# pb rows 2 to 7 as seven block products for eight, in a fp32 gated decoder step on one core

## The chip, the cores and the metric

One NeuronCore of a Trainium2 chip runs the kernel; the seven other cores are idle. The metric is device time in microseconds, from one launch. Engines are named TensorE (PE, its weight loads PEld), VectorE (DVE), ScalarE (ACT), GpSimd (POOL) and SyncE (SP, which only issues DMAs).

## The reference, cut to what matters

One layer of a hybrid decoder on 1024 prompt tokens and 8 sample tokens (T = 1032 columns), model width 1024, all in fp32:

```
z = h @ w_in;  u, v, g_a, x_b, g_b, z_a, z_b = split(z)
y_a = chunk_spatial_gate(u, rmsnorm(v)) * silu(g_a)
y_b = rg_lru(conv(x_b)) * silu(g_b)
merged = sigmoid(z_a) * (y_a @ w_pa) + sigmoid(z_b) * (y_b @ w_pb)
out = x + gate * (merged @ w_out);  y = rmsnorm(out)
```

`pb` is the product y_b @ w_pb, `pa` is y_a @ w_pa. Each is 1024 x 1024 by 1024 x 1032.

## The kernel before

Everything is held transposed: 128 channels on the partitions, 1032 tokens along the row. A fp32 operand is split in two fp32r parts, hi (a copy by ScalarE) and lo (the difference, by VectorE), and a product is three matmuls: hi·hi, hi·lo, lo·hi. Tokens lie in two halves of HT = 516 columns, each in two quarters of QW = 258.

The stages in order: the v columns of w_in; then 24 **units** (R for x_b and g_b, Z for z_a and z_b, G for u and g_a; eight of each); then pb row by row, then pa with the products of the gate between its first rows, then w_out.

A unit computes two rows of 128 output channels by a scheme with seven block products for eight: two row blocks, two halves of the contraction, two halves of the tokens. The right-hand operands of the seven products p1 to p7 are the blocks A11, A12, A22 of h and four sums S1 to S4, held in `HF`. The left-hand ones are raw weight blocks or sums of them, made by GpSimd in `sums` four stages ahead and split in `prep` two stages ahead. One product is a **stage**: `seven`, 24 matmuls of 258 columns. Results are put together by `evac` one stage later (`later`). The first unit, R0, runs its stages in another order (`FIRST`) with a fourth pair of PSUM banks.

All engines run in program order through the units (`in_order`, class `InOrder`). Side work is hung on stage numbers with `at(stage, f, ...)`: the recurrent chain (`recurrent`), the spatial gate (`spatial`), the silu's, and the spills. y_rnn(i) makes y_b's channel block i in the tile `scan_out[i, "g"]` (`gr`). For i < NSPLIT = 4 it is split at once, by y_hi in `scan_out[i]` and by y_lo in `gr` itself, and both halves are stored in DRAM as `ybs`; blocks 4 to 6 are stored whole as `ybd`; block 7 stays. Late in G7 GpSimd's queue loads the ybs tiles back, SyncE's the ybd tiles.

After the units the PSUM pool of bank pairs is closed (`new_phase`) and one of eight single banks is opened. `do_pb(m)` takes row m of pb: `product` runs three column chunks of CH = 344 with 24 matmuls each, VectorE multiplies each by sigmoid(z_b) in `sb`, and the row is stored as `mbd`. `do_pa(m)` does the same with `ya` and adds mbd's row. These rows are ordered by the list `ops`, and the weights of an op are loaded one op and split one op ahead (`fetch_load`, `fetch_split`).

SBUF tiles of one row (1032 fp32) come from one ring of NSLOT = 36 `slots`; half rows from five buffers of `half_tile`; weight blocks from `wst` (4 raw, 3 split).

Of the kernel before, what the change touches and what calls it, by code (L numbers as in the profile page):

```python
# [8 lines left out]
F32 = mybir.dt.float32  # L9
# [44 lines left out]
def tile_hybrid_step(  # L54
# [734 lines left out]
    def spill(tag):  # L789
# [21 lines left out]
    units.append(("G", KT - 1))  # L811
    pos = {u: 7 * n for n, u in enumerate(units)}
    pairs = {"R": (O_XB, O_GB), "Z": (O_ZA, O_ZB), "G": (O_U, O_GA)}
    wr, wfs = {}, {}

    def load_unit(u):
        kind, m = u
        out = []
        for j, off in enumerate(pairs[kind]):
            raw = wst[0].tile([P, 2, HD], F32, tag="raw", name=f"raw_{kind}{m}_{j}", bufs=4)  # L820
            c0 = off + m * P
            last_w[0] = S.dma_start(
                out=raw[:].rearrange("p a (k n) -> p (a k) n", n=P),
                in_=win[:, c0 : c0 + P].rearrange("(k p) n -> p k n", p=P),
            ).ins
            out.append(raw)
        wr[u] = out

    def sums(u, f):
        rx, ry = wr[u][0:2]  # L830
        first = u == units[0]
        if f == ("p4" if first else "p6"):
            t = wst[0].tile([P, 2, HD], F32, tag="wt", name=f"wt_{u[0]}{u[1]}", bufs=1)
            wr[u].append(t)
            G.tensor_tensor(t[:, 0], ry[:, 0], rx[:, 0], ALU.subtract)
            G.tensor_tensor(t[:, 1], ry[:, 1], t[:, 0], ALU.subtract)
            if first:
# [46 lines left out]
    FIRST = ("p1", "p4", "p2", "p6", "p5", "p7", "p3")  # L884
    stages = [(u, f) for u in units for f in (FIRST if u == units[0] else FORMS)]
    later = []
    side = {}

    def ahead(n, step):
        if n < len(stages):  # L890
            step(*stages[n])

    def unit(n0, u, use):
        name = f"{u[0]}{u[1]}"
        first = u == units[0]
        pa_, pb_, pc_ = (pair_bank(f"{n}_{name}") for n in "abc")
# [30 lines left out]
        for j, f in enumerate(FIRST if first else FORMS):  # L927
# [357 lines left out]
    def y_rnn(i):  # L1285
# [83 lines left out]

    def do_pb(m, w):  # L1370
        sb = slot(f"sb{m}")
        with tc.issue_after(last_w[0]):
            nc.sync.dma_start(out=sb, in_=zbd[m])
        for ps, sl in product(f"pb{m}", w, yb):
            V.tensor_tensor(sb[:, sl], ps, sb[:, sl], ALU.mult)
        nc.sync.dma_start(out=mbd[m], in_=sb)

# [18 lines left out]
    wsrc = {"pa": (w_pa[0], 0), "pb": (w_pb[0], 0)}  # L1396
    todo = list(ops)
# [22 lines left out]
    def fetch_split():  # L1420
# [3 lines left out]
        if kind == "gate":  # L1424
            hi, lo = (slot(f"gw{i}_{j}", [P, D], F32R) for j in range(2))
        elif kind == "pb" and i < 2:
            hi, lo = (slot(f"pb{i}_{j}", [P, KT, P], F32R) for j in range(2))
        else:
# [38 lines left out]
    def recurrent(i):  # L1467
# [23 lines left out]
        for t, step in zip(when, steps):  # L1491
            at(n + t, chain, i, step)
        if not last:
            at(n + 23, y_rnn, i)
        if i < NSPLIT:
# [64 lines left out]

    acts = {"pa": do_pa, "pb": do_pb, "gate": do_gate}
    for kind, i in ops:
        fetch_load()
        if (kind, i) != ("pb", 0):
            fetch_split()
        if (kind, i) == ("pb", 1):
            do_states(0, None)
        if kind == "pb" and i > 1:
            for k in {2: (0,), 3: (1,), 4: (2,), 5: (3,), 6: (4, 5), 7: (6, 7)}[i]:
                y_load("ya", yad, ya, k)  # L1570
                y_split("ya", ya, k)
        if (kind, i) == ("pa", KT - 1):
# [119 lines left out]
```

## Time and profile before

| | |
|---|---|
| median of 3 runs | 968.83 us (967.47 to 969.25) |
| the profiled execution, its own time | 965.57 us |
| its span, first to last instruction | 963.9 us |
| mean granted TensorE clock | 0.995 |
| TensorE busy | 940.5 us, 98% |
| VectorE, ScalarE, GpSimd busy | 645.2, 499.7, 228.1 us |
| units | 144.0 to 667.3 us |
| pb | 670.1 to 761.1 us |
| pa and gate products | 761.1 to 859 us |

The times below are microseconds from the start of the span of that one execution. A TensorE that is 98% busy says that nearly all other work is hidden under it; where it does wait, the profile names who released it.

### The profile page before, as it was taken

How to read it: one execution, taken by the hardware profiler on the slowest of the kernel's cores; microseconds unless marked ns; L12 is line 12 of the kernel's file. 1: busy time of each engine (PE TensorE's matmuls, PEld its weight loads, DVE VectorE, ACT ScalarE, POOL GpSimd, SP SyncE). 2: the span in 40 equal slices, each digit the busy share in tenths (PEclk: the TensorE clock that was granted, in tenths of full speed). 3: DMA queues.
4: the chain of work that ended last, by engine and by line, in shares of the span. 5: the costliest groups of instructions: out<-in, count | busy, mean ns of one | idle time of the engine just before them, and what ended most of it. 6: DMA issues, size and time to landing. Idle time of an engine off the chain costs nothing. (4 is left out here: it accounts for less than half of the span.)

```text
span 963.9 us, 16594 instructions
## 1 busy us (share of the span) xinstructions
PE 940.5 (98%) x6575; PEld 878.1 (91%) x6575; DVE 645.2 (67%) x972; ACT 499.7 (52%) x810; POOL 228.1 (24%) x170
## 2 busy tenths in 40 slices
PE   7999999999999999999999999998999999999996
PEld 3778779899999999999999999998999999997785
DVE  3886877869578587696785875969443356555544
ACT  4674446584774865846748558467122233222212
POOL 1142443233242252342422523322000000000001
PEclk9999999999999999999999999999999999999998
DMA  9952103243143163241430622518774465334321
GB/s 288 294 174 65 68 35 110 66 114 120 45 141 116 33 180 88 76 156 47 141 94 23 199 57 67 170 34 301 275 279 168 156 220 202 130 109 154 110 85 49
DMA packets 127942, 126.27 MB, mean 131 GB/s; under 512 B 10502, under 2 KB 105278, under 8 KB 127856
## 3 DMA queue, kind: packets, MB, share of 16 engines
q1 hardware_dynamic: 126648, 120.96, 39.5%
q0 software_dynamic: 1216, 4.24, 1.3%
q8 instruction: 52, 0.85, 0.4%
q14 instruction: 26, 0.21, 0.1%
HBM read 93.92 MB, written 31.33 MB: 130 GB/s over the span
## 5 line engine op out<-in xcount | busy, mean ns | idle before, releaser
L45 PE MATMUL v<-wv,h 128*128 128x512 f32 x384 | 97.1, 401 | 2.8 <-ACT junk L45 2.1
L45 PE MATMUL ps_pb<-ybh,pb 128*128 128x344 f32 x384 | 91.1, 320 | 2.8 <-issue 2.8
L45 PE MATMUL ps_pa<-yah,pa 128*128 128x344 f32 x384 | 91.4, 320 | 0.0
L45 PEld LDWEIGHTS v<-wv,h 128*128 128x128 f32 x384 | 69.6, 188 | 20.8 <-ACT junk L45 2.5
L45 POOL TENSOR_TENSOR rs_o<-ms_o,nhalf 128x1 f32<-128x1 f32 (+1 forms) x9 | 8.0, 894 | 296.3 <-DVE ms_o L45 296.3
L45 PEld LDWEIGHTS ps_pb<-ybh,pb 128*128 128x128 f32 x384 | 66.4, 188 | 3.0 <-issue 3.0
L45 PEld LDWEIGHTS ps_pa<-yah,pa 128*128 128x128 f32 x384 | 66.4, 188 | 0.5
L45 PE MATMUL ps_pb<-ybl,pb 128*128 128x344 f32 x192 | 61.4, 320 | 0.0
L45 PE MATMUL ps_pa<-yal,pa 128*128 128x344 f32 x192 | 61.4, 320 | 0.0
L45 PE MATMUL o<-wol,mgh 128*128 128x512 f32 x128 | 50.5, 395 | 0.2 <-DVE wol L45 0.2
L45 DVE SCALAR_TENSOR_TENSOR xc<-xb,vec,xc 128x512 f32<-128x512 f32 x48 | 50.3, 1049 | 0.6
L45 PE MATMUL o<-woh,mgh 128*128 128x512 f32 x128 | 50.4, 394 | 0.0
L45 PE MATMUL o<-woh,mgl 128*128 128x512 f32 x128 | 50.4, 394 | 0.0
L45 ACT ACTIVATE mgh<-sa 128x344 fp32r<-128x344 f32 x24 | 11.7, 490 | 63.2 <-DVE sa L45 59.5
L45 ACT ACT_TABLE_LOAD x34 | 43.6, 1283 | 1.4 <-PEq L1676 0.8
L45 DVE TENSOR_TENSOR sb<-ps_pb,sb 128x344 f32<-128x344 f32 x24 | 12.4, 516 | 46.3 <-PE ps_pb L45 46.3
L45 ACT ACTIVATE junk<-xr 128x512 bf16<-128x512 f32 (+2 forms) x19 | 11.6, 608 | 56.8 <-DVE xr L45 51.4
L45 POOL TENSOR_TENSOR wt_R<-raw_R,raw_R 128x512 f32<-128x512 f32 x8 | 16.9, 2106 | 97.2 <-DVE wf_Z1p L45 15.1
L45 PEld LDWEIGHTS ps_pa<-yal,pa 128*128 128x128 f32 x192 | 36.1, 188 | 0.2
L45 PEld LDWEIGHTS ps_pb<-ybl,pb 128*128 128x128 f32 x192 | 36.1, 188 | 0.0
L45 POOL TENSOR_TENSOR wt_R<-raw_R,wt_R 128x512 f32<-128x512 f32 x15 | 33.1, 2209 | 8.6 <-DVE wf_R6p L45 1.1
L45 POOL TENSOR_TENSOR wt_Z<-raw_Z,raw_Z 128x512 f32<-128x512 f32 x8 | 10.8, 1351 | 98.9 <-DVE l L45 14.2
(535 smaller groups left out, 2554.0 us busy)
## 6 DMA issues: line engine op xcount, KB each, us to landing
raw_ada<-in_w_ada_dram SPq DMA_DIRECT2D x32, 256.0 KB
raw_R<-in_w_in_dram SPq DMA_DIRECT2D x16, 512.0 KB
raw_Z<-in_w_in_dram SPq DMA_DIRECT2D x16, 512.0 KB
raw_G<-in_w_in_dram SPq DMA_DIRECT2D x16, 512.0 KB
zad<-za SPq DMA_DIRECT2D x16, 258.0 KB
yad<-t SPq DMA_DIRECT2D x8, 516.0 KB
sb<-zbd SPq DMA_DIRECT2D x8, 516.0 KB
yar<-yad SPq DMA_DIRECT2D x8, 516.0 KB
```

Source lines behind the costliest of these rows:

```text
L45: ins = f(*args, **kwargs)
```

## The change

- The eight rows of pb become four pairs. Rows 0 and 1 (unit C0) are computed in full, with 258 columns a matmul, in eight stages of 24 matmuls: four outputs (two rows, two halves) over contraction blocks 0 to 3, then the same four over blocks 4 to 7. Rows 2 to 7 (units B1 to B3) are computed as the units are, by seven products; B1 in the order of `FIRST`.
- Rows 0 and 1 of pa (unit C1) are computed as C0 is, after B3. Rows 2 to 7 of pa and the gate products stay as they are, after the change of PSUM pools, which now follows C1.
- The operands of pb are tiles of one block and one half with hi and lo side by side (`ya_tile`), and are at once A11, A12 and A22 of the seven products. `ybs` is stored in that order. S1 to S4 are new (`y_sums`, `y_form`), from fp32 blocks that are loaded back (`yb_raw`), so that ybd is stored for blocks 0 to 6; `y_lo` writes into `scan_out[i]` where it wrote into `gr`.
- Loads and splits of the operands, ya's too, are hung on stages by hand.

The diff, cut to its core:

```diff
-    ybs = { (i, j): drm.tile([P, T], ...) for i in range(NSPLIT) for j in range(2) }
+    ybs = [
+        drm.tile([P, 2, 2, HT], F32, tag=f"ybs{i}", name=f"ybs{i}") for i in range(NSPLIT)
+    ]
...
+    units += [("C", 0), ("B", 1), ("B", 2), ("B", 3), ("C", 1)]
+    pos = {}
+    for u in units:
+        pos[u] = sum(8 if v[0] == "C" else 7 for v in pos)
+    OPENERS = (units[0], ("B", 1))
...
-                x = HF[XOF[f], kp]
+                x = (YF if u[0] == "B" else HF)[XOF[f], kp]
...
+    def classical(n0, u, w, ys, use):
+        ps = [pair_bank(f"{u[0]}{u[1]}_{q}") for q in range(4)]
+        for j in range(8):
+            q, part = j % 4, j // 4
...
+            hi, lo = w[q // 2]
+            for k in range(4 * part, 4 * part + 4):
+                xh, xl = ys(k, q % 2)
...
+                    for i, (a, b) in enumerate(((hi, xh), (hi, xl), (lo, xh))):
+                        TE.matmul(ps[q][:, c, 0:QW], a[:, k % 2, ks], b[:, sl],
...
+            if part:
+                later.append(lambda q=q: use(q // 2, q % 2, ps[q][:, :, 0:QW]))
...
-        if NSPLIT <= i < KT - 1:
+        if i < KT - 1:
             later.append(lambda: S.dma_start(out=ybd[i], in_=gr))
 
     def y_hi(i):
         A.activation(scan_out[i][:].bitcast(F32R), scan_out[i, "g"], AF.Copy)
-        S.dma_start(out=ybs[i, 0], in_=scan_out[i][:])
+        S.dma_start(out=ybs[i][:, :, 0, :], in_=h2(scan_out[i][:]))
 
     def y_lo(i):
         gr = scan_out[i, "g"]
-        V.tensor_tensor(gr[:].bitcast(F32R), gr, scan_out[i], ALU.subtract)
-        S.dma_start(out=ybs[i, 1], in_=gr)
+        V.tensor_tensor(scan_out[i][:], gr, scan_out[i], ALU.subtract)
+        S.dma_start(out=ybs[i][:, :, 1, :], in_=h2(scan_out[i][:]))
...
+    def yb_parts(k):
+        for half in range(2):
+            G.dma_start(out=ya_tile(k, half), in_=ybs[k][:, half])
+    def yb_raw(k):
+        yraw[k] = slot(f"ybr{k}")
+        S.dma_start(out=yraw[k], in_=ybd[k])
+    def yb_split(k):
+        for half in range(2):
+            t = ya_tile(k, half)
+            split(t[:, 0], t[:, 1], yraw[k][:, half * HT : (half + 1) * HT])
+    def y_sums(kp, eng):
+        x, y = yraw[2 * kp], yraw[2 * kp + 1]
+        x0, x1, y0, y1 = x[:, 0:HT], x[:, HT:T], y[:, 0:HT], y[:, HT:T]
+        eng.tensor_tensor(y1, x1, y1, ALU.add)
+        eng.tensor_tensor(x1, x0, x1, ALU.subtract)
+        eng.tensor_tensor(x0, y1, x0, ALU.subtract)
+        eng.tensor_tensor(y0, y0, x0, ALU.subtract)
...
+    def pb_put(m, half, src):
+        d = sbt[m, half]
+        V.tensor_tensor(h2(d), src, h2(d), ALU.mult)
+        later.append(lambda: S.dma_start(out=mbd[m][:, half * HT : (half + 1) * HT], in_=d))
...
-    ops = [("pb", m) for m in range(KT)]
-    for m in range(KT):
-        ops += [("gate", 2 * m), ("gate", 2 * m + 1)] * (m < 4) + [("pa", m)]
+    for m in range(2, KT):
+        ops += [("pa", m)] + [("gate", 2 * m - 4), ("gate", 2 * m - 3)] * (m < 6)
...
+    c = pos["C", 0]
     for k in range(NSPLIT):
-        at(start + 1 + k // 2, yb_load2, k)
+        at(c - 6 + k // 2, yb_parts, k)
+    at(c - 4, yb_raw, 4)
+    at(c - 4, yb_raw, 5)
+    at(c - 3, yb_raw, 6)
+    at(c - 3, w_split, ("C", 0), 0)
+    at(c - 2, w_split, ("C", 0), 1)
+    at(c - 1, yb_split, 4)
+    at(c, yb_split, 5)
...
+    at(c + 1, yb_split, 6)
+    at(c + 2, yb_split, 7)
+    at(c, y_a, KT - 2)
+    at(c + 1, silu_of, t1s, KT - 1)
+    at(c + 3, y_a, KT - 1)
+    at(c - 1, yb_raw, 0)
+    at(c - 1, yb_raw, 1)
+    at(c, yb_raw, 2)
+    at(c, yb_raw, 3)
+    at(c, y_sums, 0, G)
+    at(c + 1, y_sums, 1, G)
+    at(c + 3, y_sums, 2, V)
+    at(c + 8, y_sums, 3, V)
+    for kp, t, t2 in ((0, 2, 4), (2, 4, 5), (1, 6, 10), (3, 9, 11)):
+        for j, name in enumerate(("S2", "S1", "S3", "S4")):
+            at(c + (t, t2)[j // 2], y_form, kp, name)
...
+    d = pos["C", 1]
+    for k, (a, b) in enumerate(
+        ((-9, -7), (-8, -6), (-6, -4), (-5, -3), (-4, -2), (-3, -1), (-2, 0), (-1, 1))
+    ):
+        at(d + a, y_load, "ya", yad, ya, k)
+        at(d + b, y_split, "ya", ya, k)
```

## Rows read from the trace of the kernel before

**Rows 1.** The page: busy us, share, instructions; then groups (busy, mean ns | idle).

```profile
PE 940.5 (98%) x6575; PEld 878.1 (91%) x6575; DVE 645.2 (67%) x972; ACT 499.7 (52%) x810; POOL 228.1 (24%) x170
...
L45 DVE SCALAR_TENSOR_TENSOR xc<-xb,vec,xc 128x512 f32<-128x512 f32 x48 | 50.3, 1049 | 0.6
...
L45 POOL TENSOR_TENSOR wt_R<-raw_R,wt_R 128x512 f32<-128x512 f32 x15 | 33.1, 2209 | 8.6 <-DVE wf_R6p L45 1.1
```

**Rows 2.** Waits of TensorE: us in total, times, longest.

```profile
PE ps_pb L45 <- issue: 2.8, 1, 2.8
...
PE b_R L45 <- DVE wf_R0p L45: 0.5, 1, 0.5
...
PE b_G L45 <- DVE wf_G3p L45: 0.2, 1, 0.2
```

**Rows 3.** Windows of the units and of pb: stretch, busy per engine, clock, DMA, GB/s.

```profile
240.00:647.00 407.00, 405.81 (x3375) 403.75 (x3374) 300.71 (x394) 268.04 (x399) 136.58 (x88) 1.00 0.33 98
...
670.10:761.00 90.90, 90.90 (x578) 90.84 (x579) 38.58 (x47) 21.16 (x22) 0.00 (x0) 1.00 0.66 229
```

**Rows 4.** Timeline of TensorE, first stage of Z7 and of the next unit.

```profile
580.51 3.04 PE L45 MATMUL a_Z<-h,wf_Z7p 128*128 128x258 f32 x24
...
600.61 3.05 PE L45 MATMUL a_R<-h,wf_R7p 128*128 128x258 f32 x24
```

**Rows 5.** Timeline of TensorE, pa row 0 and the gate product after it.

```profile
762.94 0.32 PE L45 MATMUL ps_pa<-yah,pa 128*128 128x344 f32 x1
...
774.30 1.99 PE L45 MATMUL pg<-gw,scp 128*41 128x512 f32 x8
```

**Rows 6.** Timeline of TensorE, last stage of G7 and first matmul of pb.

```profile
664.26 3.03 PE L45 MATMUL b_G<-h,wf_G7p 128*128 128x258 f32 x24
670.09 0.40 PE L45 MATMUL ps_pb<-ybh,pb 128*128 128x344 f32 x1 [2.81 <-issue]
```

**Rows 7.** Timeline of VectorE at the same turn.

```profile
669.30 0.69 DVE L45 TENSOR_TENSOR t<-b_G,t 128x516 f32<-128x516 f32 x1
669.91 1.29 DVE L45 TENSOR_TENSOR gr<-gr,th 128x1024 f32<-128x1024 f32 x2
```

**Rows 8.** Timeline around y_hi and y_lo of block 1: y_rnn, store, y_lo.

```profile
287.77 1.30 DVE L45 TENSOR_TENSOR gr<-gr,th 128x1024 f32<-128x1024 f32 x2
...
290.20 0.32 SPq L45 DMA_DIRECT2D ybs<-th  x1
...
291.88 1.23 DVE L45 TENSOR_TENSOR gr<-gr,th 128x1032 fp32r<-128x1032 f32 x1
...
293.03 0.69 DVE L45 TENSOR_TENSOR gr<-b_R,p_R 128x516 f32<-128x516 f32 x1
...
293.63 0.74 DVE L45 SCALAR_TENSOR_TENSOR t<-sp,vgc,wsr 128x512 f32<-128x512 f32 x1
```

**Rows 9.** Timeline, a store of one mbd row and the instruction it released.

```profile
750.52 0.33 SPq L1376 DMA_DIRECT2D mbd<-sb  x1
...
753.25 1.06 ACT L45 ACTIVATE gw<-raw_gate 128x1024 fp32r<-128x1024 f32 x1 [2.37 <-DMA mbd<-sb]
```

**Rows 10.** Timeline of TensorE, the wait in stage p7 of G1.

```profile
311.66 2.91 PE L45 MATMUL b_G<-S,wf_G1p 128*128 128x258 f32 x22 [0.22 <-DVE wf_G1p L45]
```

**Rows 11.** Timeline, GpSimd sums and the VectorE instructions beside them.

```profile
295.58 0.68 DVE L45 TENSOR_TENSOR wf_G1p<-raw_G,wf_G1p 128x512 fp32r<-128x512 f32 x1
295.59 1.81 POOL L45 TENSOR_TENSOR raw_G<-raw_G 128x512 f32<-128x512 f32 x1
...
296.18 1.77 DVE L45 SCALAR_TENSOR_TENSOR xc<-xb,vec,xc 128x512 f32<-128x512 f32 x1
...
317.37 1.28 POOL L45 TENSOR_TENSOR wt_Z<-raw_Z,wt_Z 128x512 f32<-128x512 f32 x1
317.51 1.70 DVE L45 TENSOR_TENSOR wf_Z3p<-raw_Z,wf_Z3p 128x512 fp32r<-128x512 f32 x1 [0.99 <-ACT wf_Z3p L45]
```

**Rows 12.** The tile ybs: time of its transfers on GpSimd's queue.

```profile
DMA to landing us min/median/max: 3.7/5.9/11.7
```

More of the change, by code (lines that the diff above doesn't have):

```diff
@@ L818, in load_unit @@
         out = []
+        if kind in "CB":
+            w2d = w_pa[0] if u == ("C", 1) else w_pb[0]
+            for j in range(2):
+                raw = wst[0].tile([P, 2, HD], F32, tag="raw", name=f"raw_{kind}{m}_{j}", bufs=4)
+                c0 = (2 * (0 if kind == "C" else m) + j) * P
+                for a in range(2):
+                    last_w[0] = S.dma_start(
+                        out=raw[:, a].rearrange("p (k n) -> p k n", n=P),
+                        in_=w2d[:, c0 : c0 + P].rearrange("(k a p) n -> a p k n", a=2, p=P)[a],
+                    ).ins
+                out.append(raw)
+            wr[u] = out
+            return
         for j, off in enumerate(pairs[kind]):
@@ L830, in sums @@
         rx, ry = wr[u][0:2]
-        first = u == units[0]
+        first = u in OPENERS
         if f == ("p4" if first else "p6"):
@@ L884, in tile_hybrid_step @@
     FIRST = ("p1", "p4", "p2", "p6", "p5", "p7", "p3")
-    stages = [(u, f) for u in units for f in (FIRST if u == units[0] else FORMS)]
+    stages = [
+        (u, f)
+        for u in units
+        for f in ((None,) * 8 if u[0] == "C" else FIRST if u in OPENERS else FORMS)
+    ]
     later = []
@@ L889, in ahead @@
     def ahead(n, step):
-        if n < len(stages):
+        if n < len(stages) and stages[n][1]:
             step(*stages[n])
@@ L894, in unit @@
         name = f"{u[0]}{u[1]}"
[L895 removed]
+        first = u in OPENERS
         pa_, pb_, pc_ = (pair_bank(f"{n}_{name}") for n in "abc")
@@ new lines, in y_form, with sb_load @@
+    def y_form(kp, name):
+        x, y = yraw[2 * kp], yraw[2 * kp + 1]
+        src = {"S1": y[:, HT:T], "S2": x[:, 0:HT], "S3": x[:, HT:T], "S4": y[:, 0:HT]}[name]
+        t = YF[name, kp] = slots.tile([P, 2, HT], F32R, tag="s", name=f"y{name}_{kp}")
+        split(t[:, 0], t[:, 1], src)
+    sbt = {}
+    def sb_load(m, halves_):
+        if halves_:
+            for half in range(2):
+                t = sbt[m, half] = half_tile(f"sb{m}_{half}")[:]
+                S.dma_start(out=t, in_=zbd[m][:, half * HT : (half + 1) * HT])
+            return
+        t = slot(f"sb{m}")
+        S.dma_start(out=t, in_=zbd[m])
+        for half in range(2):
+            sbt[m, half] = t[:, half * HT : (half + 1) * HT]
@@ L1368, in y_split, with pa_load, pa_put @@
         out[k] = (yh, yl)
[L1370 to L1376, printed above, removed]
+    pat = {}
+    def pa_load(m):
+        sa, mb = slot(f"sa{m}"), slot(f"mb{m}")
+        S.dma_start(out=sa, in_=zad[m])
+        S.dma_start(out=mb, in_=mbd[m])
+        pat[m] = sa, mb
+        mg.append((slot(f"mgh{m}", dt=F32R), slot(f"mgl{m}", dt=F32R)))
+    def pa_put(m, half, src):
+        sa, mb = pat[m]
+        mh, ml = mg[m]
+        sl = slice(half * HT, (half + 1) * HT)
+        V.tensor_tensor(h2(sa[:, sl]), src, h2(sa[:, sl]), ALU.mult)
+        V.tensor_tensor(sa[:, sl], sa[:, sl], mb[:, sl], ALU.add)
+        split(mh[:, sl], ml[:, sl], sa[:, sl])
+        sv_ = q4(sa)[:, 2 * half : 2 * half + 2, QP:QW]
+        hv = [
+            hsp[:, m, c + 4 * half : c + 4 * half + 4].rearrange("p (q x) -> p q x", q=2)
+            for c in (0, 32)
+        ]
+        split(hv[0], hv[1], sv_)
     def do_pa(m, w):
@@ L1425, in fetch_split @@
             hi, lo = (slot(f"gw{i}_{j}", [P, D], F32R) for j in range(2))
-        elif kind == "pb" and i < 2:
-            hi, lo = (slot(f"pb{i}_{j}", [P, KT, P], F32R) for j in range(2))
+        elif i == 2:
+            hi, lo = (slot(f"pa{i}_{j}", [P, KT, P], F32R) for j in range(2))
         else:
@@ L1492, in recurrent @@
             at(n + t, chain, i, step)
-        if not last:
-            at(n + 23, y_rnn, i)
+        at(n + 23 - 2 * last, y_rnn, i)
         if i < NSPLIT:
@@ L1536, in tile_hybrid_step @@
             load_unit(units[n + 1])
-        unit(7 * n, u, users[u[0]](u[1]))
+        if u == ("C", 0):
+            classical(
+                pos[u],
+                u,
+                cw[u],
+                lambda k, half: (YA[k, half][:, 0], YA[k, half][:, 1]),
+                lambda j, half, src: pb_put(j, half, src),
+            )
+        elif u == ("C", 1):
+            classical(
+                pos[u],
+                u,
+                cw[u],
+                lambda k, half: [y[:, half * HT : (half + 1) * HT] for y in ya[k]],
+                lambda j, half, src: pa_put(j, half, src),
+            )
+        else:
+            unit(pos[u], u, users[u[0]](u[1]))
     for step in later:
```

96 lines of the change are left out of this document (58 added, 38 removed).

## The prediction

> **What bounds the kernel now.** I read first the busy times of the engines: TensorE is busy 940.5 of 963.9 us, VectorE 645.2, ScalarE 499.7 [rows 1]. Then the waits of TensorE: after the start-up the largest is 2.8 us, where pb begins, and those inside the units that matter below are 0.2 us each [rows 2]. So the time is the sum of TensorE's instructions plus its few gaps, and a change is worth what it takes from either. The granted clock is 1.00 in every stretch that the change touches [rows 3], so no part of the forecast is a clock effect.
>
> Then the timeline of TensorE, for the price of a matmul in each form. Unit Z7 (seven stages of 24 matmuls, 258 columns) runs from 580.51 to 600.61 [rows 4]: 20.10 us, 2.871 us a stage, 119.6 ns a matmul. One output row of pa (72 matmuls, 344 columns) runs from 762.94 to 774.30 [rows 5]: 11.36 us, 157.8 ns a matmul. 96 matmuls of 258 columns do the same columns as 72 of 344 and cost 11.49 us for 11.36: the narrower form is dearer by 0.12 us a row.
>
> **The change part by part.** *Products.* pb rows 2 to 7 become three units of seven stages: 3 x 20.10 = 60.30 us for 6 x 11.36 = 68.16, which is -7.86. pb rows 0, 1 and pa rows 0, 1 stay in full, in eight stages of 24 matmuls each: 22.97 for 22.72, twice, which is +0.50. Sum: **-7.36 us**. Bounds from the same rows are a tenth of a us either way.
>
> *The turn from the units to pb.* G7's last stage begins at 664.26, its columns end near 667.3, and pb's first matmul starts at 670.09 after 2.81 us [rows 6]. VectorE is what is late there: it evacuates p4, whose columns it could have had at 667.3, from 669.30 to 669.99, and TensorE starts 0.10 us later [rows 7]. The old code closes the PSUM pool at this point. In the new code the first product of pb comes in the same phase and takes banks that were freed earlier, and the late p4 evacuation is wanted only by the fourth stage, 8 us later: **-2.8**. The pool is closed after C1 instead. There VectorE has little to do, so the gap is the last evacuation alone, a multiplication of 0.69 us (the same shape as p4's evacuation) [rows 7] and about 0.2 around it: **+0.9**. Bounds 0 (the first bank is an early one) and +2.8 (as now).
>
> *The four y_lo.* This is the part that I expect to take back some of the gain. Now y_lo writes its low half over `gr`. `gr` must now survive, since ybd wants it in fp32, so y_lo writes over `scan_out[i]`, which the DMA of the high half, issued one stage before, is still reading. VectorE works in order, so it stands until that store is done. For i = 1 the store is issued at 290.20 and y_lo starts at 291.88 [rows 8]. How long a 516 KB store from SP's queue takes shows once: an mbd store issued at 750.52 released ScalarE at 753.25, 2.73 us after [rows 9]. Then y_lo can't start before 292.93: 1.05 us late. Behind it on VectorE stand the evacuations and weight splits of the next unit, in an unbroken row of work, and TensorE has no slack at its end: in G1's stage p7 TensorE already waits 0.22 for the split of its weights [rows 10]; the same wait is there in G2 and G3 (three in all, one shown in [rows 2]), each behind a y_lo. Some of it comes back: a 512-wide multiply-add took 1.77 us beside a GpSimd sum [rows 11] where the mean of its kind is 1.05 [rows 1], and GpSimd, not delayed, would be done before it: 0.7. Left is 0.35. But the new ybd store of the same tile, which for i < 4 was not there, goes out as soon as `gr` is final, at 289.07 [rows 8], 1.1 us ahead of the high half in the same queue, and may delay it by up to what is then left of its own 2.73, 1.6: between 0.35 and 1.95. I take 0.6, near the lower end, since little else moves there: **4 x 0.6 = +2.4**. Bounds: 0 (all of it absorbed) and 4 x 1.95 = +7.8.
>
> The Trainium skill, "DMA: Bandwidth & Descriptors", section on the anatomy of one DMA, gives a transfer about 2.0 us of fixed cost, mostly the receipt at the target memory, plus its bytes at 436 GB/s: an estimate of 3.2 us for 516 KB. By that figure the wait is 1.5, what is left 0.8, the four cost 3.3 for 2.4, and the sum below would be -5.7; the trace's 2.73 was on this very queue, so the row decides.
>
> *Operands of the product by sevens.* New work falls between stages c - 3 and c + 11 (c: first stage of C0): 16 forms split on ScalarE and VectorE, four groups of four sums (two on GpSimd, two on VectorE), yb splits by halves, four more 516 KB loads. The question is whether VectorE reaches the split of B1's first weights in time. Up to y_rnn(7), at 669.91 now [rows 7], it has as much to do as before: two weight splits and one yb split for two yb splits and one weight split. From there, by start spacings of 0.60 us for 516 wide (293.03 to 293.63) and 1.15 for 1032 wide (291.88 to 293.03) [rows 8]: y_rnn 1.2, two y_a 2.3, three yb splits 3.6, eight forms 4.8, one group of sums 2.4, two evacuations 1.2, the split 0.6 = 16.1, so 686.0. B1 starts at 667.3 + 22.97 = 690.2: 4.2 us to spare. Behind the loads of raw 0 to 3, which I put at 668, GpSimd's eight sums and then B1's three weight sums take 11 x 1.8 (1.28 to 1.81 each in [rows 11], 2.2 as the dearest mean [rows 1]): done by 688, at 2.2 each by 692, and the p4 weights are wanted at 693.1. Both fit, so I take **+0.3** for small waits, as R0, the one unit now in this order, shows at its own start with 0.5 [rows 2]. Bounds 0 and +4 (below).
>
> *Covered at no cost.* The ya loads and splits move from pb into B2 and B3, where VectorE has some 8.4 us of work in 20 (seven splits and about seven evacuations of 0.6); sb, sa and mb loads are issued 4 stages ahead of use; gates keep two rows of pa (22.7 us) between the last gate and the residuals that want gbc. If that cover failed, one late ya costs at most its load, about 3 us.
>
> *Sum:* -7.36 - 2.8 + 0.9 + 2.4 + 0.3 = **-6.56**. On the profiled execution's own 965.57 us (span 963.9) that is 959.0. The runs' median is 968.83, 0.34% above the profiled one; the difference is carried over: **962.3**. What a measurement here can tell from no change is about 0.2%, 1.9 us.
>
> **Rivals.** *The stores stack (R1).* ybd's store delays the high half by 0.6 to 1.6, so four times 0.95 to 1.95, +3.8 to +7.8 for +2.4: the sum is -5.2 to -1.2, near 965.6. For it: VectorE's unbroken row and TensorE's missing slack [rows 8, 10]. Against: at 1.1 us apart the two would overlap for the most part, if a store's 2.73 is mostly delay and not bandwidth.
>
> *VectorE is late at B1 (R2).* A VectorE split of 512 columns took 1.70 us beside a GpSimd sum that had begun before it, and 0.68 where it began first (295.58) [rows 11]. If each of the eight GpSimd sums holds VectorE by 1.0, the 4.2 us to spare become -3.8, and the three weight sums add up to 3: TensorE waits 4 to 7, the sum is -2.9 to 0, near 967.4. It decides from 0.5 us a sum on. For it: VectorE is full there, so each sum meets one. Against: it takes the loss on nearly every sum; at 295.58 it was the GpSimd sum that grew, to 1.81 [rows 11]. The Trainium skill, "SBUF — State Buffer", section on the two separate sides, says that a VectorE instruction with two SBUF inputs and a GpSimd one lock each other out for a whole instruction, whichever comes first; both pairs of rows agree with it, and it is the mechanism of this rival.
>
> *Stores land late: slower (R3).* Transfers of the same size from the other queue took 3.7 at least, 5.9 in the median [rows 12]. With 5.9 for the high half, y_lo starts at 296.1, 4.2 late, 3.5 after what comes back; four times is 14.0 for 2.4: +5.0, 973.9. It decides from a landing of 4.6 us on (8.96 / 4 + 0.7 late). Against: those loads came eight in a row into full DMA engines; around the stores little else moves.
>
> *The full gain.* If y_lo is absorbed and the new gap is small: -10.2 to -9, near 959.3.
>
> **How the numbers follow.** Forecast with its own spread (-10.2 to -4, the full gain within it): 0.62. R1 0.14, 0.11 of it faster and 0.03 within 0.2%. R2 0.13, 0.05 faster and 0.08 within. R3 0.08, slower. 0.03 for a late buffer or load that I don't see, 0.02 of it slower. Faster 0.62 + 0.11 + 0.05 = 0.78; same 0.03 + 0.08 + 0.01 = 0.12; slower 0.10. The range: 958.6 (all lower bounds) up to 967.8, which takes in R1 and most of R2 and leaves R3 out. The likeliest case's own range is 958.6 to 964.8.
>
> **What the profile would show.** Right: no gap of TensorE between G7 and C0; B units of 20.1 us; a gap near 0.9 before pa row 2; in R1 to R4 VectorE idle about 1 us before y_lo, released by a DMA, and p7 waits in G0 to G3 grown from 0.2 to 0.6 or more. Wrong: TensorE waits at the start of B1 or its third and fourth stages, released by VectorE or GpSimd (R2); y_lo waits of 3 us and more (R3); waits of SP for buffers between G7 and B1 that make raw 0 to 3 late.

## The result, and the profile after

The changed kernel took 972.72 us (median of 5 runs, 971.42 to 974.52), the kernel before beside it 967.99 (5 runs, 966.02 to 969.25): ratio 1.0052, 95% interval 1.0037 to 1.0067. It is slower, by 4.7 us. The forecast was 962.3 and faster. The profiled execution took 972.72 with a span of 971.0, 7.1 more than the 963.9 of before; below, spans are compared. The profiled execution of before was one of its quick ones (965.57 for a median of 967.99), so the spans differ by more than the medians do.

TensorE's timeline of the changed kernel, from the last unit to C1 (start, duration, instruction and count, and in brackets the idle time before it with its releaser):

```profile
650.29 3.05 PE L45 MATMUL a_G<-h,wf_G7p 128*128 128x258 f32 x24
...
669.38 3.03 PE L45 MATMUL b_G<-h,wf_G7p 128*128 128x258 f32 x24
672.25 14.02 PE L45 MATMUL C<-yp,wC 128*128 128x258 f32 x115
688.06 11.03 PE L45 MATMUL C<-yp,wC 128*128 128x258 f32 x77 [1.79 <-DVE yp L45]
702.40 0.48 PE L45 MATMUL a_B<-yp,wf_B1p 128*128 128x258 f32 x2 [3.30 <-ACT yS L45]
704.72 5.10 PE L45 MATMUL a_B<-yp,wf_B1p 128*128 128x258 f32 x22 [1.84 <-DVE wf_B1p L45]
...
722.29 3.14 PE L45 MATMUL b_B<-yS,wf_B1p 128*128 128x258 f32 x24 [0.90 <-ACT u_B L45]
...
728.15 3.07 PE L45 MATMUL a_B<-yp,wf_B2p 128*128 128x258 f32 x24
...
768.46 0.28 PE L45 MATMUL C<-yah,wC 128*128 128x258 f32 x1
...
791.47 0.28 PE L45 MATMUL C<-yah,wC 128*128 128x258 f32 x1
791.59 0.32 PE L45 MATMUL ps_pa<-yah,pa 128*128 128x344 f32 x1
```

Read it from stage to stage. The 2.81 us between G7 and pb [rows 6] are gone: C0 begins at 672.25, 2.87 after G7's last stage, one stage's length. B2 and B3 take 728.15 to 768.46, 40.31 us, twice 20.15. C1 takes 23.1, and pa row 2 follows it without a gap. But G7 begins at 650.29, where it began at 645.21 before, and C0 with B1 takes 672.25 to 728.15: 55.90 us where 22.97 + 20.10 = 43.07 were due. The four waits in the brackets are 7.83 us of that excess of 12.83. The rest is in TensorE's clock; the windows of the same stretch (busy time by engine with counts, granted clock, DMA share, GB/s):

```profile
687.00:690.00 3.00, 1.94 (x14) 1.94 (x15) 3.00 (x3) 0.00 (x0) 2.92 (x3) 0.90 0.45 165
690.00:693.00 3.00, 3.00 (x16) 3.00 (x16) 3.00 (x2) 0.00 (x0) 2.84 (x3) 0.53 0.00 0
693.00:696.00 3.00, 3.00 (x27) 3.00 (x26) 3.00 (x3) 0.00 (x0) 3.00 (x2) 1.00 0.00 0
...
702.00:705.00 3.00, 0.76 (x3) 0.58 (x4) 3.00 (x6) 1.40 (x3) 0.00 (x0) 0.68 0.25 96
705.00:708.00 3.00, 3.00 (x15) 3.00 (x16) 3.00 (x6) 0.00 (x0) 0.00 (x0) 0.50 0.81 246
```

At 690 to 693 TensorE is busy throughout and yet issues 16 matmuls where it issues 27 at a granted clock of 1.00; at 705 to 708 the clock is at 0.50, the lower of the two levels, 1.2 GHz. Set against their counts, C0's 192 matmuls lose 1.9 us so and B1's 168 lose 2.9.

What the waits wait for stands on VectorE, and what holds VectorE on GpSimd. VectorE's timeline in C0:

```profile
675.06 3.27 DVE L45 TENSOR_TENSOR gr<-gr,th 128x1024 f32<-128x1024 f32 x2
678.25 2.39 DVE L45 TENSOR_TENSOR yp<-ybr,yp 128x516 fp32r<-128x516 f32 x2
...
682.82 3.50 DVE L45 TENSOR_TENSOR yp<-ybr,yp 128x516 fp32r<-128x516 f32 x2
686.25 3.47 DVE L45 TENSOR_TENSOR yp<-gr,yp 128x516 fp32r<-128x516 f32 x2
689.64 3.46 DVE L45 TENSOR_TENSOR yS<-ybr,yS 128x516 fp32r<-128x516 f32 x2
...
695.26 1.77 DVE L45 TENSOR_TENSOR ybr<-ybr,ybr 128x516 f32<-128x516 f32 x1
...
703.99 0.68 DVE L45 TENSOR_TENSOR wf_B1p<-raw_B,wf_B1p 128x512 fp32r<-128x512 f32 x1
```

and GpSimd's, where `ybr` is written by the sums of y and `wt_B` by the sums of B1's weights:

```profile
674.77 1.29 POOL L45 TENSOR_TENSOR ybr<-ybr,ybr 128x516 f32<-128x516 f32 x1 [13.95 <-DMA ybr<-ybd]
...
678.38 5.69 POOL L45 TENSOR_TENSOR ybr<-ybr,ybr 128x516 f32<-128x516 f32 x3
...
689.12 1.73 POOL L45 TENSOR_TENSOR wt_B<-raw_B,raw_B 128x512 f32<-128x512 f32 x1
...
694.21 2.27 POOL L45 TENSOR_TENSOR raw_B<-raw_B 128x512 f32<-128x512 f32 x1
```

A split of 516 columns that starts 0.60 after the one before it when GpSimd is still [rows 8] starts 1.7 after it here: 3.50 for two. From 675.06 to 697.03 VectorE ends 13 instructions; at their free spacings (0.60 for 516 or 512 wide, 1.15 for 1032) they are 8.9 us of work, and they took 22.0: 1.0 us lost on each. GpSimd's sums run from 674.77 to 696.5, the whole of that stretch. The Trainium skill, "SBUF — State Buffer", section "SBUF: two separate sides", describes an exclusive lock between such a pair of instructions; the 3.50 for two beside GpSimd agrees with it.

The other loss, G7's late start, comes in the units where block 0 to 3 is split. From G0's first matmul to G4's it is 234.1 to 494.4 before, 260.3 us, and 234.3 to 499.4 after, 265.1. TensorE's waits there (us in total, times, longest) show it where [rows 2] had 0.2 each:

```profile
PE b_G L45 <- ACT wf_G3p L45: 0.6, 1, 0.6
PE b_G L45 <- ACT wf_G2p L45: 0.6, 1, 0.6
...
PE b_G L45 <- DVE wf_G2p L45: 0.2, 1, 0.2
```

and VectorE at block 1's y_lo, with SyncE's two stores ahead of it and the GpSimd sum beside it (rows of three engines' timelines):

```profile
290.24 0.32 SPq L45 DMA_DIRECT2D ybd<-gr  x1
291.34 6.18 SPq L45 DMA_DIRECT2D ybs<-th  x2
...
294.56 1.30 POOL L45 TENSOR_TENSOR wt_G<-raw_G,wt_G 128x512 f32<-128x512 f32 x1
...
294.70 2.24 DVE L45 TENSOR_TENSOR th<-gr,th 128x1032 f32<-128x1032 f32 x1 [1.60 <-DMA ybs<-th]
```

The high part's store was issued at 291.34 and released y_lo at 294.70, 3.36 us after; y_lo, 1.23 long before [rows 8], then took 2.24, because a GpSimd sum had begun 0.14 ahead of it.

### The profile page after: what moved, and what is told of

The parts are those of the page before. It is cut to its first block, busy times and chain, and to the rows that moved or that the text cites. A ratio compares the mean times of both kernels' runs of the same rounds, so it can differ in the third digit from the quotient of the medians.

```text
span 971.0 us, 17159 instructions
## 1 busy us (share of the span) xinstructions
PE 939.9 (97%) x6743; PEld 875.8 (90%) x6743; DVE 685.0 (71%) x1013; ACT 518.7 (53%) x855; POOL 259.3 (27%) x190
## 5 line engine op out<-in xcount | busy, mean ns | idle before, releaser
L45 PE MATMUL ps_pa<-yah,pa 128*128 128x344 f32 x288 | 68.9, 320 | 0.0
L45 PEld LDWEIGHTS ps_pa<-yah,pa 128*128 128x128 f32 x288 | 49.8, 188 | 0.4
L45 ACT ACTIVATE mgh<-sa 128x344 fp32r<-128x344 f32 (+1 forms) x22 | 11.3, 516 | 68.7 <-DVE sa L45 64.4
L45 PE MATMUL ps_pa<-yal,pa 128*128 128x344 f32 x144 | 46.0, 319 | 0.0
L45 ACT ACTIVATE r<-rg,vec 64x516 f32<-64x516 f32 x32 | 21.9, 683 | 21.2 <-PE rg L45 21.1
L45 POOL TENSOR_TENSOR wt_G<-raw_G,wt_G 128x512 f32<-128x512 f32 x16 | 24.1, 1507 | 30.6 <-DVE wf_G2p L45 5.0
L45 ACT ACTIVATE h<-ht,sv,av 128x128 fp32r<-128x128 f32 (+2 forms) x33 | 17.5, 557 | 27.2 <-PE ht L45 18.7
L45 POOL TENSOR_TENSOR wt_G<-raw_G,raw_G 128x512 f32<-128x512 f32 x8 | 10.4, 1294 | 79.5 <-DVE wf_G6p L45 13.6
L45 PEld LDWEIGHTS o<-woh,mgh 128*128 128x128 f32 x128 | 24.0, 188 | 5.7
L45 PEld LDWEIGHTS o<-wol,mgh 128*128 128x128 f32 x128 | 24.0, 188 | 5.6 <-DVE wol L45 0.2
```

Of the source, the lines that this page charges most:

```text
L45: ins = f(*args, **kwargs)
```

## The experiments

Thirteen kernels. **Theory:** the loss in C0 and B1 is VectorE held by GpSimd's sums (rival R2, deeper than priced), the loss in the units is y_lo's wait. **Rivals:** the new operands are simply too much work for the time ahead of B1; the falling clock is the loss; y_lo's wait costs nothing and something else in the units does. Each kernel is a version of the changed one, except E3. "C0 + B1" is from C0's first matmul to B2's, "G0 to G4" from G0's first to G4's; the ratio is to the kernel before on the same chip. Medians are of 4 to 10 runs but for E5.

| run | edit | median us | ratio (95%) | G0 to G4 | C0 + B1 |
|---|---|---|---|---|---|
| before | | 966.95 to 967.99 | 1 | 260.3 | |
| changed | | 972.72 | 1.0052 (1.0037 to 1.0067) | 265.1 | 55.90 |
| E1 | sums of y on VectorE | 969.29 | 1.0017 (1.0004 to 1.0031) | 264.3 | 52.92 |
| E2 | y_lo into a free tile | 968.99 | 1.0015 (1.0002 to 1.0028) | 260.3 | 55.32 |
| E3 | before, y_lo into the busy tile | 967.23 | 0.9997 (0.9984 to 1.001) | 260.9 | |
| E4 | E1 and E2 | 965.61 | 0.9972 (0.9958 to 0.9986) | 260.2 | 51.56 |
| E5 | E2, no sums at all | 956.21, one run | | | 44.35 |
| E6 | E4, splits ahead of sums | 965.25 | 0.9976 (0.9962 to 0.9989) | 260.2 | 52.10 |
| E7 | E6, B1's weight sums on VectorE too | 963.68 | 0.9967 (0.9953 to 0.9981) | 260.3 | 50.14 |
| E8 | E4, two pairs by sevens for three | 960.13 | 0.9926 (0.99 to 0.9953) | 260.2 | |
| E9 | fp32 store behind y_lo's | 973.8 | 1.0067 (1.0047 to 1.0088) | 264.3 | 55.0 |
| E10 | TensorE's idle time filled | 975.84 | 1.0091 (1.0073 to 1.0109) | 265.2 | 58.6 |
| E11 | E8, its sums on GpSimd | 961.38 | 0.9933 (0.9916 to 0.995) | 260.3 | |
| E12 | whole rows stored | 970.33 | 1.0036 (1.0022 to 1.0051) | 262.1 | 55.7 |
| E13 | filled in B1 only | 975.67 | 1.0096 (1.0079 to 1.0114) | 265.2 | 58.2 |

**E1, the lock alone.** The eight sums of y that GpSimd does go to VectorE, which thereby gets 5.7 us more work (the two groups take 2.89 and 2.79 us in E7, where GpSimd is still).

```diff
-    at(c, y_sums, 0, G)
-    at(c + 1, y_sums, 1, G)
+    at(c, y_sums, 0, V)
+    at(c + 1, y_sums, 1, V)
```

> The two groups of sums for S1 to S4 that GpSimd makes are put on VectorE. Theory (GpSimd's sums hold VectorE up: splits of 516 columns beside them take 1.7 us for 0.7): VectorE gets 4.8 us more work, but every split is back at 0.6 to 0.7; the stretch C0 and B1, 55.9 us in the changed kernel, shrinks to 45 to 48, and the time falls by 8 to 11, to 962 to 965. Rival (VectorE simply has too much to do there, whoever makes the sums): the 4.8 us come on top, 975 to 978. Second rival (the fp32 blocks are loaded too late for any engine): the stretch stays as it is, 972 to 973.

C0 and B1 became 3.0 us shorter, 52.92 for 55.90, although the engine that is late was given work: eight instructions on GpSimd had cost VectorE more than doing them itself. The 45 to 48 us expected were not reached: B1's four weight sums stayed on GpSimd and now ran beside the first group of y's sums, which took 5.7 us on VectorE (679.91 to 685.63), where the second, alone, took 2.8. TensorE's waits (us in total, times, longest) are now ahead of parts of y, which stand behind the sums in VectorE's order, and for B1's `u_B`:

```profile
PE C L45 <- DVE yp L45: 3.7, 2, 3.0
PE b_B L45 <- ACT u_B L45: 2.0, 1, 2.0
```

**E2, y_lo's target.** y_lo writes into a tile of the gates that is dead by then, so no store holds it.

```diff
-        V.tensor_tensor(scan_out[i][:], gr, scan_out[i], ALU.subtract)
-        S.dma_start(out=ybs[i][:, :, 1, :], in_=h2(scan_out[i][:]))
+        lo = gates[i][1]
+        V.tensor_tensor(lo[:], gr, scan_out[i], ALU.subtract)
+        S.dma_start(out=ybs[i][:, :, 1, :], in_=h2(lo[:]))
```

> y_lo writes its low half into the tile ig, which is dead by then, and so has no store to wait for. Theory (the wait for the store of the high half sets TensorE back in R1 to R4): the units are 5.1 us shorter, G7 starts at 645 as before, C0 and B1 stay at 56 us: 967 to 968. Rival (the ybd stores or the 2064-byte pieces of ybs set the units back, not the wait): 971 to 973.

G0 to G4 is back at 260.3 us: the whole 4.8 us that the units lost was this one wait and what followed from it.

**E3, the wait without the rest.** The kernel before, with y_lo's target as in the change; its stores are whole rows, and no fp32 store is ahead.

```diff
-        V.tensor_tensor(gr[:].bitcast(F32R), gr, scan_out[i], ALU.subtract)
-        S.dma_start(out=ybs[i, 1], in_=gr)
+        V.tensor_tensor(scan_out[i][:].bitcast(F32R), gr, scan_out[i], ALU.subtract)
+        S.dma_start(out=ybs[i, 1], in_=scan_out[i][:])
```

> The kernel before, with one edit: y_lo writes into scan_out instead of gr; no ybd store for blocks 0 to 3, ybs in its old form. Theory (the wait is for the landing of the high half, 2.7 us after its issue): VectorE waits about 1.05 us in each of four, without the store ahead of it; TensorE loses 0.5 to 1 us each, G7 starts 2 to 4 us later: 970 to 972. Rival (only the store ahead makes it long): under 0.2 us each, 968 to 969.

Its timeline at the same place, the store and y_lo:

```profile
290.31 4.57 SPq L45 DMA_DIRECT2D ybs<-th  x2
...
293.09 1.45 DVE L45 TENSOR_TENSOR th<-gr,th 128x1032 fp32r<-128x1032 f32 x1 [1.02 <-DMA ybs<-th]
```

The wait is there, 1.02 us where the prediction had worked out 1.05, and TensorE hardly feels it: 0.54 us over four blocks, not the 0.5 to 1 a block that was expected, and no change in the median. So the change's 1.6 us is not that wait with a little more on it; it is on the far side of a step. Two things differ from E3: the fp32 store ahead, and `ybs` written by halves. E9 and E12 take them apart.

**E9, the store ahead.** The fp32 store goes out behind the low part's.

```diff
         if i < KT - 1:
-            later.append(lambda: S.dma_start(out=ybd[i], in_=gr))
+            if i >= NSPLIT:
+                later.append(lambda: S.dma_start(out=ybd[i], in_=gr))
...
         S.dma_start(out=ybs[i][:, :, 1, :], in_=h2(scan_out[i][:]))
+        S.dma_start(out=ybd[i], in_=gr)
```

> The changed kernel, with one thing moved: for blocks 0 to 3 the store of the fp32 block (516 KB) is issued after the store of the block's low part, not before the store of its high part. If the wait of 1.6 us of each y_lo in the changed kernel is the high part's store standing behind the fp32 block's store, then y_lo waits about 1.0 us as it did where only the high part was stored (the kernel before with the same target of y_lo), PE loses little in units G0 to G3 and unit G7 begins at 645.5 to 646.5 instead of 650.3; C0 and B1 stay at 55 to 56 us, and the median comes to 967.5 to 969.5. The rival: the wait lasts as long because the high part's transfer itself takes that long, the stretch still ends near 650, and the median stays at 972 to 973.

The theory of that run fell. Its timeline:

```profile
292.41 6.17 SPq L45 DMA_DIRECT2D ybs<-th  x2
...
295.62 1.29 POOL L45 TENSOR_TENSOR wt_G<-raw_G,wt_G 128x512 f32<-128x512 f32 x1
...
295.70 2.29 DVE L45 TENSOR_TENSOR th<-gr,th 128x1032 f32<-128x1032 f32 x1 [1.53 <-DMA ybs<-th]
```

With nothing ahead of it the store still took 3.29 us, y_lo still came just behind a GpSimd sum, and G0 to G4 was 264.3.

**E12, the pieces.** `ybs` is laid out by parts, each a row of 4128 B per partition; the halves are picked out at the load. The fp32 store stays ahead.

```diff
-    drm.tile([P, 2, 2, HT], F32, tag=f"ybs{i}", name=f"ybs{i}")
+    drm.tile([P, 2, T], F32, tag=f"ybs{i}", name=f"ybs{i}")
...
-        S.dma_start(out=ybs[i][:, :, 0, :], in_=h2(scan_out[i][:]))
+        S.dma_start(out=ybs[i][:, 0, :], in_=scan_out[i][:])
...
-            G.dma_start(out=ya_tile(k, half), in_=ybs[k][:, half])
+            G.dma_start(out=ya_tile(k, half), in_=ybs[k][:, :, half * HT : (half + 1) * HT])
```

> The changed kernel with the buffers of the split blocks laid out by parts (high part, low part, each a whole row of 4128 B per partition) instead of by halves (pieces of 2064 B); the stores of the fp32 blocks stay ahead, and the loads pick the halves out of the two rows. If the longer landing of the high part's store (3.3 us from its issue, with the fp32 store ahead of it or behind it, against 2.8 us where the kernel before stored whole rows) comes from the pieces, the wait of y_lo falls from 1.6 to about 1.0 us, its collision with GpSimd's sums goes, and unit G7 begins at 645.5 to 647 instead of 650.3: median 967.5 to 970. The rival: the store ahead or the low part's target makes the wait whatever the pieces are; G7 stays near 650 and the median at 972 to 974.

```profile
290.74 4.61 SPq L45 DMA_DIRECT2D ybs<-th  x2
...
293.77 1.23 DVE L45 TENSOR_TENSOR th<-gr,th 128x1032 f32<-128x1032 f32 x1 [1.26 <-DMA ybs<-th]
...
293.96 2.19 POOL L45 TENSOR_TENSOR wt_G<-raw_G,wt_G 128x512 f32<-128x512 f32 x1
```

Now y_lo starts 0.19 ahead of the GpSimd sum, and it is the sum that grows, to 2.19. Not so at every block. At block 2 of this run the same store took 3.74 us, and y_lo came behind the sum again:

```profile
359.30 1.29 POOL L45 TENSOR_TENSOR wt_G<-raw_G,wt_G 128x512 f32<-128x512 f32 x1
359.83 1.85 DVE L45 TENSOR_TENSOR th<-gr,th 128x1032 f32<-128x1032 f32 x1 [1.98 <-DMA ybs<-th]
```

At block 3 of E9 the two started together, and y_lo was not held:

```profile
428.47 1.23 DVE L45 TENSOR_TENSOR th<-gr,th 128x1032 f32<-128x1032 f32 x1 [1.45 <-DMA ybs<-th]
428.47 2.38 POOL L45 TENSOR_TENSOR wt_G<-raw_G,wt_G 128x512 f32<-128x512 f32 x1
```

What G0 to G4 loses against the 260.3 of before goes by how many of the four y_lo begin behind this sum (the second of the unit's weight sums, `wt_G<-raw_G,wt_G`): none in E3, 0.5 us; one in E12, 1.8; three in E9 and in E1, 4.0; four in the changed kernel, 4.8, and in E10, 4.9. The sum begins 3.2 us after the store is issued (changed kernel, E9), so the step lies there. From issue to release, over the four blocks: whole rows alone 2.71 to 2.78 (E3); whole rows behind the fp32 store 2.93 to 3.03, once 3.74 (E12); halves alone 3.22 to 3.29 (E9); halves behind it 3.22 to 3.57 (changed). The pieces are the larger part: they alone bring three of the four blocks over the step. The store ahead adds nothing to the halves that can be told, since E1, which has it, lost what E9 lost. With whole rows it may have brought the one block; E3's rows also lie without gaps in DRAM and E12's do not, and no run takes these two apart. The median came to 970.33, just over the 970 expected at most: the loss in the units is not all gone. The Trainium skill, "DMA: Bandwidth & Descriptors", section "Specifications", gives 512 B as the least transfer for the full rate; pieces of 2064 B landed 0.5 us later here than whole rows of 4128 B (E9 beside E3), so above that size too the piece counted.

**E4, both repairs.** E1's and E2's edits together.

> Both edits: all sums for S1 to S4 on VectorE, and y_lo into ig. Theory: the two losses lie in different stretches and add up; 13 to 16 us off the changed kernel: 957 to 960, 0.8 to 1.1% under the kernel before. Rival (TensorE set back 5 us less leaves VectorE 5 us less to get ready for B1): part of it comes back as a longer C0 and B1: 961 to 965.

965.61: the two gains, 0.35 and 0.37% alone, add up to 0.80%. The kernel is now faster than before, by 0.28%, but short of the 957 to 960 expected: C0 and B1 still take 51.56 for 43.07.

**E5, no sums.** E2 without the sixteen sums, so that rows 2 to 7 of pb are computed from wrong operands; it is for its time alone.

```diff
-    at(c, y_sums, 0, G)
-    at(c + 1, y_sums, 1, G)
-    at(c + 3, y_sums, 2, V)
-    at(c + 8, y_sums, 3, V)
```

> As e2_lo_ig, with the sixteen sums for S1 to S4 left out: the forms are split from the fp32 blocks themselves, so rows 2 to 7 of pb are not the reference's. Theory (the sums, their time on VectorE and what GpSimd's hold up, are what C0 and B1 wait for): without them VectorE has 11 us less to do and no sum of GpSimd beside it but B1's weight sums; C0 and B1 take 43.5 to 46 us for 55.3, without a drop of the clock: 957 to 960. Rival (the late loads of the blocks, or the forms alone, keep it): over 50 us.

C0 and B1 fell to 44.35, with one wait of 0.9 for `u_B`, at a clock of 1.00 from 672 to 712. So everything else that was added to this stretch (loads, forms, splits, parts) is covered; the sums, on either engine, are 7.2 us (E4) to 11 us (E2) of its length.

**E6 and E7, the order and the rest of GpSimd.** E6 is E4 with the sums behind the splits of y's parts; E7 is E6 with the sums of B1's weights on VectorE as well.

```diff
-    at(c, y_sums, 0, V)
-    at(c + 1, y_sums, 1, V)
+    at(c + 2, y_sums, 0, V)
+    at(c + 5, y_sums, 1, V)
...
+            E = V if u == ("B", 1) else G
-            G.tensor_tensor(t[:, 0], ry[:, 0], rx[:, 0], ALU.subtract)
+            E.tensor_tensor(t[:, 0], ry[:, 0], rx[:, 0], ALU.subtract)
```

(The second part is E7's alone; the other three sums of the unit go the same way.)

> As e4_both, with the sums moved behind the splits that C0 waits for: the first group from stage c to c + 2, the second from c + 1 to c + 5. Theory (VectorE is overbooked between c and c + 11; the order only decides where TensorE stands): the waits of 0.8 and 3.0 us in C0 go, B1 waits 2 to 4 us instead; C0 and B1 48 to 50 us for 51.6, time 962 to 965. Rival (only the order was wrong): no wait over 1 us, 44 us, 957 to 959.

> As e6_splits_first, with B1's four weight sums on VectorE too, so that no sum of GpSimd runs between G7 and B2's. Theory (each GpSimd sum costs VectorE more than the sum itself would): VectorE gets 2.4 us more work and loses 3 to 4 us of standing still: 1 to 2 us better than e6_splits_first. Rival (work is work): 1 to 3 us worse.

E6's median is that of E4, and C0 and B1 take 52.10 us, not the 48 to 50 expected; the wait left C0 and came back ahead of B1, 4.6 us for `wf_B1p`. E7 gave 2 us of C0 and B1, again by giving VectorE more to do; its median came 1.6 lower, the ratio's interval overlaps E6's. None of these orders makes VectorE's work fit: with GpSimd silent, 3.8 us of wait remain.

**E8 and E11, later instead of sooner.** E4 with rows 2 and 3 of pb in full too (unit C2), so that the first sevens begin 23 us after C0's end instead of at it; the sums are spread over c + 4 to c + 13. E11 is E8 with all sixteen sums on GpSimd.

```diff
-    units += [("C", 0), ("B", 1), ("B", 2), ("B", 3), ("C", 1)]
+    units += [("C", 0), ("C", 2), ("B", 2), ("B", 3), ("C", 1)]
...
-    at(c, y_sums, 0, V)
-    at(c + 1, y_sums, 1, V)
-    at(c + 3, y_sums, 2, V)
-    at(c + 8, y_sums, 3, V)
+    at(c + 4, y_sums, 0, V)
+    at(c + 9, y_sums, 1, V)
+    at(c + 6, y_sums, 2, V)
+    at(c + 13, y_sums, 3, V)
```

> As e4_both, with rows 2 and 3 of pb in full as well, by eight stages after C0, and only rows 4 to 7 by seven products; the sums and forms are spread over the 23 us that this gives (sums at c + 4, 6, 9, 13, forms from c + 9 to c + 19). It gives up 2.87 us of products. Theory (VectorE's load in the stretch is the cause): C0, C2 and the first unit by sevens take 66 to 68 us without a wait over 1 us and with the clock at 1.00; time 958 to 961. Rival (something else makes C0 long, the loads or the ring of slots): waits as in e4_both, 967 to 969.

> The version with two pairs in full and two by sevens (960.1), with its four groups of sums of y on GpSimd instead of VectorE; the groups begin at the same stages. If GpSimd's sums only hurt where VectorE has no slack, VectorE's operations beside them grow from about 0.7 to 1.7 us and PE hardly waits, because the operands are due twenty stages later than in the changed kernel: 959.5 to 961.5. The rival: the lock costs more than the slack of this order, waits for parts of y come back in C0 and C2, and it takes 963 or more.

E8, 960.13 us, is the fastest, 0.74% below before: it gives up one pair's saving (22.97 for 20.10) and gets most of the operands' loss back, 5.5 us under E4, which has the same repairs. C0, C2 and B2 take 67.45 for 66.04, and in TensorE's waits from 640 to 740 only one of all those for operands of pb is left:

```profile
PE b_B L45 <- ACT u_B L45: 0.9, 1, 0.9
```

The window of the turn (busy time by engine, clock, DMA):

```profile
672.00:700.00 28.00, 28.00 (x235) 28.00 (x235) 23.73 (x28) 6.38 (x10) 6.28 (x4) 1.00 0.68 223
```

VectorE is busy 23.7 of 28 us, where in the changed kernel it was 27.9, and the clock stays at 1.00. In E11 the lock is all there again, in VectorE's timeline:

```profile
675.52 3.50 DVE L45 TENSOR_TENSOR yp<-ybr,yp 128x516 fp32r<-128x516 f32 x2
678.94 3.47 DVE L45 TENSOR_TENSOR yp<-gr,yp 128x516 fp32r<-128x516 f32 x2
```

and in TensorE's waits it costs one:

```profile
PE C L45 <- DVE yp L45: 1.5, 1, 1.5
```

E8 and E11 can't be told apart. The same 3.50 for two splits that set the end in the changed kernel is nearly free where the operands are due a unit later.

**E10 and E13, the clock.** Products of no use in TensorE's idle time: 15 in C0 ahead of its wait and 44 ahead of B1 (E10), or 27 and 15 ahead of B1's first two stages (E13). In E10 they stand in PSUM banks that blocks of pb share and disturb the values of such a block.

```diff
+                if u == ("C", 0) and j == 4 and k == KT - 1:
+                    fill(15, hi, ps[1])
...
+            if u == ("B", 1) and f == "p1":
+                fill(44, cw["C", 0][1][0], pd_)
```

> The changed kernel with matrix products of no use put into the two places of C0 and B1 where PE idles: 15 of them ahead of the last block's products of C0's stage 4, 44 ahead of B1's first stage; they write columns of PSUM that nothing reads. If some 5 us of the 12.8 us that C0 and B1 lose are the granted clock, which falls to 0.50 to 0.73 after the waits, the clock stays at or near 1.00 from 688 to 712, the operands come at the same times, and C0 with B1 takes 50 to 52 us instead of 55.9: 967 to 969. The rival: VectorE's lateness sets the end whatever the clock is, the time saved on products goes into longer waits, and the median stays at 972 to 973.5.

> The changed kernel with matrix products of no use only in B1: 27 ahead of its first stage and 15 ahead of its second, in banks of PSUM that are free by then and are overwritten by the stage itself (3.2 and 1.8 us of products at full clock, about the length of the two waits there). If the clock's fall to 0.50 in B1 is a loss of its own, B1's stages run at 1.00, the waits of 3.3 and 1.8 us go into the filling, and C0 with B1 takes 53 to 54 us instead of 55.9, the median 969.5 to 971. The rival, which the run with filling ahead of B1 and in C0 already bears out for C0: VectorE's lateness sets the end, the time goes into other waits, and the median stays at 972 to 974.

In C0 the filling did what it was to do: no wait, 1.00 throughout, C0's last matmul over at 697.7, 25.0 us after its first where the changed kernel took 26.8. Nothing came of it: both kernels are slower than the changed one, and above the range of either expectation. E10's timeline of TensorE:

```profile
672.69 25.03 PE L45 MATMUL C<-yp,wC 128*128 128x258 f32 x207
702.95 7.22 PE L45 MATMUL d_B<-yp,wC 128*128 128x252 f32 x44 [5.23 <-DVE sb L45]
```

and its windows after C0:

```profile
699.00:702.00 3.00, 0.00 (x0) 0.00 (x0) 2.97 (x6) 2.77 (x6) 0.00 (x0) 0.69 0.00 0
702.00:705.00 3.00, 2.05 (x9) 2.05 (x10) 3.00 (x6) 2.04 (x4) 0.00 (x0) 0.50 0.23 88
```

The time gained went into the next wait, 5.23 for 3.30. Every version with three pairs by sevens and the first sums on GpSimd starts B1's first stage 29.8 to 30.4 us after C0: 30.15 in the changed kernel, where the clock fell in C0; 30.37 in E2, 29.9 in E9 and E12 and 30.26 in E10, where it did not. VectorE sets that point, and the clock's fall in C0 adds nothing to it that can be told. Ahead of B1 neither filling answers the question: its PSUM banks come free only with VectorE's multiplications (`sb`), so that the filling waited there too, 5.23 and 4.77 us, met the low clock itself (E13's 27 products took 5.3 us, 3.2 at full clock) and lengthened the path. What the fall in B1 costs by itself was not isolated; by the counts it is 2.9 us in the changed kernel and goes together with the wait, as E5 and E8 show no fall.

## Why the prediction was wrong

*Right.* The products: B2 and B3 20.15 us each, C0's and C1's stages as priced where the clock held, -7.4. The turn: -2.8, with C0 behind G7 without a gap. The last term there was too high: between C1 and pa row 2 there is no gap (791.47 to 791.59 is one matmul) for +0.9, which is the lower bound given.

*The failed step* is "Operands of the product by sevens": +0.3 forecast, +12.8 measured, far above its bound of +4. It counted VectorE's work at free spacings, 16.1 us up to B1's first split, and found 4.2 us to spare; GpSimd's sums it counted only for when they themselves would be done. In place of 0.60 a split took 1.7, and thirteen instructions in a row lost 1.0 us each. Without these 13.1 us the split of B1's first weights, over at 704.67, would be over at 691.6 (an estimate from these rows), 3.6 us ahead of the end of C0's products at full clock, 695.2: the count of VectorE's own work held, and what it left out is the price of GpSimd's beside it. The mechanism was on record as R2, with the right place, rows and sign, at a chance of 0.13, and "it takes the loss on nearly every sum" was held against it. But where VectorE has no idle time and GpSimd runs one sum behind another, every instruction meets one: that is what happened, 13.1 us where R2 took 8 + 3. R2's 4 to 7 us of waits became 6.9 (the 0.9 for `u_B` stays even without sums, E5), and 4.8 came on top from the granted clock, which the prediction had excluded because it was 1.00 in [rows 3]: rows of a stretch without waits say nothing of one with them. The 1.9 of it that fell in C0 stand in the place of waiting: where the clock held there, the waits were 8.0 us (E9) and 7.9 (E12), and C0 with B1 took 55.0 and 55.7. It had also the raw blocks at 668; the first pair's sums began at 674.77, as soon as the DMA had landed, which put them on the last parts of y as well as on the sums behind.

*The four y_lo*: +2.4 forecast, +4.8 measured. Sign and place were right, and the wait without the fp32 store, worked out as 1.05, measured 1.02 (E3). The size was wrong twice. That wait, taken as 0.35 a block, costs 0.15; the wait of 1.6, a mere 0.6 longer, costs 1.2, since y_lo then starts behind a GpSimd sum and itself takes 2.24 for 1.23. And the cause of the longer wait was sought in the store ahead (R1), where the halves in which the same bytes are written, in the diff but not priced, are the larger part (E9, E12). The 1.5 us that the prediction also worked out, from a fixed cost and a rate (figures for GpSimd's queue, while this store is on SyncE's), came near the 1.6 by luck: whole rows took 2.71 to 2.78 for its 3.2, and the rest is the halves'.

*The sum*: -7.4 - 2.8 + 0.3 (B2, B3 and C1 over their price) + 4.8 + 12.8 = +7.7. Measured, w_out starts 8.0 us later (859.21 before, 867.19 after), and the span is 7.1 longer, since what follows came out 0.9 shorter; the rest lies in small differences.

## What to carry to other kernels

Price an instruction of VectorE by what GpSimd does at the same time: on an engine with no idle time each GpSimd sum beside it cost 1.0 us here, more than the instruction itself, and handing work from the full engine to the idle one can make the full one later; moving the sums to the late engine gave 3 us. When new operands have to be made ahead of a faster product, count the slack from the moment their inputs have landed, and give the slow form one unit more before the fast one begins: here two pairs by sevens with time to prepare beat three without, at the same repairs (960.1, E8, to 965.6, E4). A store whose end frees a buffer is to be priced by its pieces and not by its bytes alone, and a wait that is free at 1.0 us may not be at 1.6.

## What the runs showed of the hardware that was not expected

- Stores of 516 KB from SyncE's queue: 2.71 to 2.78 us from issue to release in rows of 4128 B (E3), 3.22 to 3.29 in pieces of 2064 B (E9), with no store ahead of either; a store of the same size issued 1.1 us earlier left it at 3.22 to 3.57 in pieces (changed kernel).
- A start 0.14 us behind or 0.19 us ahead of a GpSimd sum decides which of the two takes 1 us longer: y_lo 2.24 and the sum 1.30, or y_lo 1.23 and the sum 2.19. Counted over the four blocks, this alone sorts what the units lost in six kernels, from 0.5 to 4.9 us.
- The granted clock fell to 0.50 around waits of 3.3 to 5.2 us ahead of B1. In C0 it fell after a wait of 1.79 in the changed kernel, but not after one of 2.01 in E2, nor in the kernel before after the 2.81 of [rows 6]: the length of a wait alone did not decide it.
